# Holding the exponentials, and some row steps, while a gate bank's sums end, and spacing the copies of rpb

## The chip, the core and the metric

The kernel runs on one core of a Trainium2 chip. The core has a matrix engine (TensorE, PE in the profile; its weight loads are PEld), VectorE (DVE), ScalarE (ACT), GpSimd (POOL) and SyncE (SP), whose queue issues most transfers, and 16 DMA engines that the queues share. Each engine takes its instructions in program order and waits at one whose inputs are not there. The metric is the device time of one execution in microseconds, the median of several runs.

## The reference

One trunk layer is applied to 128 context tokens and 256 latent tokens, with the same weights and different conditioning:

```python
h = rms_norm(x, n1) * (1 + sc1) + sh1
q, k, v, u = project_in(h, w_in, q_g, k_g)       # 2048 -> 3*1024 + 1024
attn = attend(q, k, v)                           # 16 heads of 64
na = attn @ w_na_proj
fn = fourier_mix(u) @ w_fnet_proj
g_na, g_fn = split(sigmoid(h @ w_gate))          # 2048 -> 4096
x = x + g1 * ((g_na * na + g_fn * fn) @ w_o)
h2 = rms_norm(x, n2) * (1 + sc2) + sh2
x = x + g2 * swiglu(h2, w_gate_up, w_down)       # d_ff 5632
```

The shifts, scales and gates (sh1 to g2) come from silu(cond) @ w_mod, 2048 to 12288 wide. Context tokens attend to the context; latent tokens lie on a grid of 4 rows by 64 columns and attend, in one softmax, to a window of that grid with a bias table rpb, and to 128 cached keys. Keys and values of the context are outputs too.

## The kernel before, in words

**Products.** All weights are float32. A product of two float32 matrices is made as three matmuls of rounded halves (`mm3`, L147 to L149): high with high, high with low, low with high. Weights come in units of 256 rows by 512 columns: a load on SP's queue (`load_unit`, L187), then a split (`split`, L143 and L144): ScalarE casts the high half `wh`, VectorE subtracts it for the low half `wl`. `next_unit` gives the unit that is multiplied now; the unit that it splits is used two units later. `wh` and `wl` have three buffers each, the raw loads four.

**Work beside the products.** Everything else is written as generators which `Paced` steps at a rate per tick. `next_unit` has two ticks. The first one steps what is in the list `front`; then the split of a weight unit is issued; the second one steps `front` and `behind`. Inside the gate stage `mid_unit` gives a third tick to `front`, between the products of f = 0, 1 and those of f = 2, 3. I call the three A, B and C. Since all engines work in program order, the place of a step between these ticks sets its place in every engine's queue: what is issued on tick A stands ahead of the unit's split, what is issued on B or C stands behind it.

**Stages.** First come the modulation sums and the projection w_in in four groups of units (up to about 350 us). In the last group every unit multiplies for all tokens and the sums of a chunk of 512 columns are added up in SBUF (`acc`, L682); the sums of q, k, v, u go to DRAM (`s_qkvu`, written by `after`, L624 to L648). At the start of this group `expand_rpb` is put in `behind`: seven transfers from DRAM to DRAM (L250), each of which writes a slice of rpb 64 times over, so that the bias of a head pair can later be read as a slanted view (`bp`, L843).

Then comes the gate stage (about 350 to 690 us): eight banks of four sums (`po`, one PSUM tile for 128 gate columns by 384 tokens), each over eight units (u = 0, 2, ... 14). While the last unit is multiplied, each finished sum is copied to SBUF (`gst`, L1032): f = 0 and 1 on VectorE if one of the last three attention ticks held exponentials (`soft`), else on ScalarE; f = 2 and 3 on ScalarE. Four transfers on ScalarE's queue (L1035) store them. The next bank's first matmul needs the PSUM tile that the first copy frees.

Beside the gate products run, in `front`, the Fourier mixing and then the attention, in eight head pairs, and the row steps. The order of a pair is the table PAIR, fifteen ticks, that is five units:

```python
PAIR = "qk,b,pv,s0 m0,e0 i0,lq,s1 m1,e1 i1,,t0 lb,v,,t1,lv,"
```

`qk` transposes and splits q and k (L860 to L878), `b` masks the bias (L882), `pv` makes the products with v of the pair before (L976, L979, then L987 and L988), `s` makes scores (matmuls L893; then L905 on VectorE for the latent keys and L910, L914 on ScalarE for the others), `m` the maxima (L920, L924, VectorE), `e` the exponentials with their sums (L932, ScalarE), `i` the reciprocals (L940, VectorE) and the scaling (L942, ScalarE), `t` transposes (L958, TensorE) and splits (`pt`), `v` splits the values (L966, L967), and `lq`, `lb`, `lv` issue loads for the next pair. The digit is the tile of queries; s0 has four blocks of keys for each head pair to exponentiate, s1 two.

**Row steps.** Another part of the modulation is multiplied on VectorE: `accr` (L327, L329) takes one row block `wmr` of w_mod (loaded at L299) and adds it, times silu(cond), to a sum. `rows.rate` sets the steps per tick, and `rows.least` how much must be due before a tick does any.

Of the kernel before, what the change touches and what calls it, by code (L numbers as in the profile page):

```python
# [14 lines left out]
F32R = mybir.dt.float32r  # L15
# [4 lines left out]
P = 128  # L20
D = 2048
KT = D // P
# [79 lines left out]
def trunk_kernel(ctx: ExitStack, tc: tile.TileContext, io: dict):  # L102
# [35 lines left out]
    def nm(s):  # L138
        return f"{s}{next(ids)}"
# [6 lines left out]
    def mm3(out, aH, aL, bH, bL, start, stop):  # L146
        nc.tensor.matmul(out, aH, bH, start=start, stop=False)  # L147
        nc.tensor.matmul(out, aH, bL, start=False, stop=False)  # L148
        nc.tensor.matmul(out, aL, bH, start=False, stop=stop)  # L149

    def warm_sqrt():

        warm = small.tile([P, 1], F32, tag="warm", bufs=1, name=nm("warm"))
        nc.scalar.activation(out=warm, in_=ones[:, 0:1], func=AF.Sqrt)
# [53 lines left out]
    def next_unit():  # L208

        for p in front:  # L210
            p.tick()
        split_unit()
        for p in front + behind:
            p.tick()
        loads.more()
        return ready.popleft()
# [9 lines left out]
    qg8 = consts.tile([P, 1], F32, tag="qg8", name="qg8")  # L226
    rq = consts.tile([P, NT, NH], F32, tag="rq", name="rq")

    hH = [None] * KT
    hL = [None] * KT  # L230

    def new_h(kt):
        hH[kt] = hpool.tile([P, TOK], F32R, tag=f"tH{kt}", name=nm(f"hH{kt}_"))
        hL[kt] = hpool.tile([P, TOK], F32R, tag=f"tL{kt}", name=nm(f"hL{kt}_"))
        return hH[kt], hL[kt]

    s_qkvu = [dram.tile([P, NT, CH], F32, tag=f"sq{i}", name=f"s_qkvu{i}") for i in range(8)]
# [9 lines left out]
    def expand_rpb():  # L247
        for i in range(7):
            src = bass.AP(io["rpb"].tensor, (4 + i) * 31 + 15 - 63, [[465, NH], [0, 64], [1, P]])
            nc.sync.dma_start(s_rpb[i], src)  # L250
            yield
# [14 lines left out]
    with ExitStack() as ph:  # L266
# [170 lines left out]
        with ExitStack() as pha:  # L437
# [214 lines left out]
            for gi, (k0, n) in enumerate(GROUPS):  # L652
                prep.due, prep.rate = DUE[gi], PREP[gi]
                prep.least = 3.6 if gi else 1
                if gi == len(GROUPS) - 1:
                    behind.append(Paced(expand_rpb()))
                    new_ring()
                for rate, ci in zip(CHUNKS, ORDER):
                    if gi == len(GROUPS) - 1:
                        rows.rate = rate  # L660
                    po = [(mm_tile if gi < len(GROUPS) - 1 else acc_tile)() for _ in range(NT)]
                    if gi == 0:
                        acc[ci] = c6([P, NT, CH], "acc")
                    for u in range(k0, k0 + n, 2):
                        wH, wL = next_unit()
                        while prepared[0] < min(u + 2, k0 + n):
                            prep.step()
                        for t in range(NT):
                            sl = slice(t * P, (t + 1) * P)
                            for kk in range(min(k0 + n - u, 2)):  # L670
                                mm3(
                                    po[t], hH[u + kk][:, sl], hL[u + kk][:, sl], wH[:, kk], wL[:, kk],
                                    u + kk == k0, u + kk == k0 + n - 1,
                                )
                            if u + 2 >= k0 + n:
                                a = acc[ci][:, t]
                                if gi == 0 and t < 2:
                                    nc.scalar.copy(a, po[t])
                                elif gi == 0:
                                    nc.vector.tensor_copy(a, po[t])  # L680
                                else:
                                    nc.vector.tensor_add(a, a, po[t])  # L682
                    if gi == len(GROUPS) - 1:
                        behind.append(Paced(after(ci)))
# [128 lines left out]
                values()  # L813

        qks, vs, biases = [], [], []
        soft = deque(maxlen=3)

        def load_qk(hp):
# [27 lines left out]
        def attention_pair(hp, wk, values_before):  # L846
# [151 lines left out]
                    ("s", scores), ("m", maxima), ("e", exps), ("i", inverses), ("t", keys_first))},  # L998
            }
            for tick in PAIR.split(","):  # L1000
                for w in tick.split():
                    work[w]()
                soft.append("e" in tick)
                yield
# [13 lines left out]
        for fc8 in range(8):  # L1018
            po = [mm_tile() for _ in range(4)]
            sts = []  # L1020
            for u in range(0, KT, 2):
                wH, wL = next_unit()
                for f in range(4):
                    s = slice(f * P, (f + 1) * P)
                    if f == 2:
                        mid_unit()
                    for kk in range(2):
                        k = u + kk
                        mm3(po[f][:, :TOK], wH[:, kk, s], wL[:, kk, s], hH[k], hL[k], k == 0, k == KT - 1)
                    if u == KT - 2:  # L1030
                        st = gst.tile([P, TOK], F32, tag="st", name=nm("gst"))
                        (nc.vector.tensor_copy if f < 2 and any(soft) else nc.scalar.copy)(st, po[f][:, :TOK])  # L1032
                        sts.append(st)
            for f, st in enumerate(sts):
                nc.scalar.dma_start(s_gate[fc8][:, f], st)  # L1035
        br_work.drain()
        front.clear()
        behind.append(rows)
        pha.close()
# [368 lines left out]
```

## Time and profile before

| | |
|---|---|
| median of three runs | 2050.86 us (2049.79 to 2052.56) |
| profiled execution | 2052.19 us, span of the profile 2050.4 us |
| granted TensorE clock | 0.998 |
| TensorE busy, first 55 us | 41.95 us |
| TensorE busy, 55 to 350 us (w_in) | 291.82 of 295 us |
| TensorE busy, 350 to 700 us (gates, attention) | 346.80 of 350 us |
| VectorE busy, 350 to 700 us | 283.03 us |
| ScalarE busy, 350 to 700 us | 197.47 us |
| TensorE busy, 860 us to the end | 1186.01 of 1190 us |

A busy share says how much an engine works, not whether it is late. For that one reads the waits (who stood idle, and what instruction ended that) and the timeline, whose rows give start and duration in us, the engine, the line, the operation, and in brackets the idle time just before with its releaser.

### The profile page before, as it was taken

To read this page: it belongs to the slowest core of one execution; us is meant where nothing else is said; L and a number is where in the kernel's file an instruction comes from. 1 tells how busy PE (TensorE), PEld (TensorE's weight loads), DVE (VectorE), ACT (ScalarE), POOL (GpSimd) and SP (SyncE) were. 2 spreads that over 40 slices of the span, in tenths; PEclk is the share of its full clock that TensorE was granted. 3 is DMA by queue.
4 is the path that set the end of the run, shared out by engine and by line. 5 is a ranking of instruction groups with operands and counts; after the bars stand their busy time and mean duration, and the time that the engine had idled before them with its cause. 6 is when DMAs were issued, how large, how long until landed. Compare 5 with 4: busy or idle time off the path is not lost.

```text
span 2050.4 us, 27528 instructions
## 1 busy us (share of the span) xinstructions
PE 2025.8 (99%) x10986; PEld 1843.8 (90%) x10986; DVE 1248.0 (61%) x1528; ACT 757.9 (37%) x1135; POOL 43.1 (2%) x92
## 2 busy tenths in 40 slices
PE   7999999999999999999999999999999999999999
PEld 4668788999999999889998999899989998999897
DVE  4746889788987777765854444545454334333456
ACT  4433232456665434334523332222222232223222
POOL 1000000000001000010000000000000000000000
PEclk9999999999999999999999999999999999999999
DMA  9996979677776776754455555455554444444453
GB/s 332 328 338 222 309 232 315 215 217 212 228 212 181 258 248 194 250 168 154 124 167 156 152 163 155 144 153 155 155 163 134 124 129 127 129 128 123 136 163 123
DMA packets 220384, 390.46 MB, mean 190 GB/s; under 512 B 28464, under 2 KB 77632, under 8 KB 220256
## 3 DMA queue, kind: packets, MB, share of 16 engines
q1 hardware_dynamic: 213088, 382.13, 59.5%
q10 hardware_dynamic: 4672, 6.31, 0.9%
q8 instruction: 86, 1.41, 0.3%
q0 software_dynamic: 2496, 0.27, 0.1%
q14 instruction: 42, 0.34, 0.1%
HBM read 371.81 MB, written 20.51 MB: 191 GB/s over the span
## 4 chain that ended last, share of the span: by engine, by line
PE 94%; DMA 3%; DVE 2%; ACT 1%; issue 0%; SPq 0%; ACTq 0%; DVEq 0%
PE mm L147 19%; PE mm L149 19%; PE mm L148 19%; PE at L147 11%; PE at L149 11%; PE at L148 11%; PE at L404 1%; DMA wm<-in_w_mod 1%; DMA wraw<-in_w_in 1%; PE at L893 1%; PE at L979 1%; PE at L958 1%; DMA wmr<-in_w_mod 1%; DVE accr L329 0%; DMA xc<-in_x_prompt 0%
## 5 line engine op out<-in xcount | busy, mean ns | idle before, releaser
L144 DVE TENSOR_TENSOR wl<-wraw,wh 128x1024 fp32r<-128x1024 f32 (+1 forms) x464 | 559.1, 1205 | 668.5 <-ACT wh L143 667.3
L143 ACT CAST wh<-wraw 128x1024 fp32r<-128x1024 f32 (+1 forms) x464 | 480.9, 1038 | 1032.0 <-PE at L148 272.9
L147 PE MATMUL mm<-hH,wh 128*128 128x384 f32 x1152 | 389.4, 338 | 2.4 <-DVE gst L1032 2.4
L149 PE MATMUL mm<-hH,wl 128*128 128x384 f32 x1152 | 385.5, 335 | 0.0
L148 PE MATMUL mm<-hL,wh 128*128 128x384 f32 x1152 | 385.2, 334 | 0.0
L329 DVE SCALAR_TENSOR_TENSOR accr<-wmr,csz,accr 128x1024 f32<-128x1024 f32 x240 | 304.8, 1278 | 5.2 <-DMA wmr<-in_w_mod 5.1
L147 PEld LDWEIGHTS mm<-hH,wh 128*128 128x128 f32 x1152 | 216.3, 188 | 8.1 <-issue 4.3
L148 PEld LDWEIGHTS mm<-hL,wh 128*128 128x128 f32 x1152 | 216.4, 188 | 0.0
L149 PEld LDWEIGHTS mm<-hH,wl 128*128 128x128 f32 x1152 | 216.2, 188 | 0.0
L147 PE MATMUL at<-hH,wh 128*128 128x384 f32 x640 | 213.9, 334 | 0.0
L149 PE MATMUL at<-hH,wl 128*128 128x384 f32 x640 | 213.9, 334 | 0.0
L148 PE MATMUL at<-hL,wh 128*128 128x384 f32 x640 | 213.8, 334 | 0.0
L147 PE MATMUL mm<-wh,hH 128*128 128x512 f32 x404 | 160.8, 398 | 1.9 <-ACT hH L548 1.2
L148 PE MATMUL mm<-wl,hH 128*128 128x512 f32 x404 | 158.1, 391 | 2.8 <-DVE wl L144 2.8
L149 PE MATMUL mm<-wh,hL 128*128 128x512 f32 x404 | 158.4, 392 | 0.7 <-DVE hL L144 0.4
L147 PE MATMUL mm<-wh,cH 128*128 128x512 f32 x352 | 137.1, 389 | 0.0
L149 PE MATMUL mm<-wh,cL 128*128 128x512 f32 x352 | 137.0, 389 | 0.0
L148 PE MATMUL mm<-wl,cH 128*128 128x512 f32 x352 | 137.0, 389 | 0.0
L147 PEld LDWEIGHTS at<-hH,wh 128*128 128x128 f32 x640 | 120.1, 188 | 1.0 <-ACT wh L143 0.8
L148 PEld LDWEIGHTS at<-hL,wh 128*128 128x128 f32 x640 | 120.1, 188 | 0.2
L149 PEld LDWEIGHTS at<-hH,wl 128*128 128x128 f32 x640 | 120.1, 188 | 0.0
L147 PEld LDWEIGHTS mm<-wh,hH 128*128 128x128 f32 x404 | 76.0, 188 | 25.6 <-issue 3.1
(283 smaller groups left out, 2633.5 us busy)
## 6 DMA issues: line engine op xcount, KB each, us to landing
wraw<-in_w_gate_up SPq DMA_DIRECT2D x176, 512.0 KB, 3.7
wmr<-in_w_mod SPq DMA_DIRECT2D x128, 512.0 KB, 4.9
wraw<-in_w_down SPq DMA_DIRECT2D x88, 512.0 KB, 3.7
wraw<-in_w_gate SPq DMA_DIRECT2D x64, 512.0 KB, 4.3
wm<-in_w_mod SPq DMA_DIRECT2D x80, 384.0 KB, 6.7
wraw<-in_w_in SPq DMA_DIRECT2D x56, 512.0 KB, 5.8
wraw<-in_w_o SPq DMA_DIRECT2D x32, 512.0 KB, 4.7
wraw<-in_w_fnet_proj SPq DMA_DIRECT2D x16, 512.0 KB, 4.9
```

Source lines behind the costliest of these rows:

```text
L143: nc.scalar.copy(H, x)
L144: nc.vector.tensor_sub(L, x, fr(H))
L147: nc.tensor.matmul(out, aH, bH, start=start, stop=False)
L148: nc.tensor.matmul(out, aH, bL, start=False, stop=False)
L149: nc.tensor.matmul(out, aL, bH, start=False, stop=stop)
L329: nc.vector.scalar_tensor_tensor(out=acc[:, cnd], in0=wm, scalar=sc, in1=acc[:, cnd], op0=ALU.mult, op1=ALU.add)
L404: nc.tensor.matmul(pm[q : q + 32, :w], csz[:, k, :], wm[:, ty, kk + par, :], start=k < 2, stop=k >= KT - 2, tile_position=(0, q), skip_gro ...
L893: nc.tensor.matmul(po[j][:, cols], qx[rows[j], q], kx[rows[j], k], start=i == 0, stop=i == 2, tile_position=(j * HD, 0),)
L958: nc.tensor.transpose(o[:, i * P : (i + 1) * P], sc[:, j, c0 : c0 + P], ident)
L979: nc.tensor.matmul(po[j][:, CTX:TOK].rearrange("p (t q) -> p t q", t=2), w[1 + kc], x.rearrange("p (t b) q -> p t b q", t=2)[:, :, 2 * kc ...
```

## The change

It has three parts. The table of ticks, the rates and all the arithmetic are the same.

1. The transfers of `expand_rpb` are paced at 0.2 steps a tick, so that one goes every fifth unit and not one in each of the first seven.
2. While a bank's last unit (u = 14) is issued, `ending` is set. A tick of the attention that holds exponentials then yields instead, and comes at the first tick at which the flag is off, ahead of which no later step of the attention can go. In the same unit `rows.least` is 3, so that row steps wait; it is 1 again with the next unit and after the stage.
3. The high and low half of h share one tile of 2 x 384 columns. `hx`, a flat view of that tile, and `mm3_wide`, a product over it, are defined and not used.

```diff
+    def mm3_wide(out, aH, aL, b, start, stop):
+
+
+        nc.tensor.matmul(out, aH, b[:, :CH], start=start, stop=False)
+        nc.tensor.matmul(out[:, CH - TOK : TOK], aH, b[:, CH:], start=False, stop=False)
+        nc.tensor.matmul(out[:, :TOK], aL, b[:, :TOK], start=False, stop=stop)
+
...
+    hx = [None] * KT
     hH = [None] * KT
     hL = [None] * KT
 
     def new_h(kt):
-        hH[kt] = hpool.tile([P, TOK], F32R, tag=f"tH{kt}", name=nm(f"hH{kt}_"))
-        hL[kt] = hpool.tile([P, TOK], F32R, tag=f"tL{kt}", name=nm(f"hL{kt}_"))
+        h = hpool.tile([P, 2, TOK], F32R, tag=f"t{kt}", name=nm(f"h{kt}_"))
+        hH[kt], hL[kt] = h[:, 0], h[:, 1]
+        hx[kt] = h.rearrange("p i t -> p (i t)")
         return hH[kt], hL[kt]
...
-                    behind.append(Paced(expand_rpb()))
+                    behind.append(Paced(expand_rpb(), 0.2))
...
+        ending = [False]
         soft = deque(maxlen=3)
...
             for tick in PAIR.split(","):
+                while ending[0] and "e" in tick:
+                    yield
                 for w in tick.split():
                     work[w]()
                 soft.append("e" in tick)
...
             for u in range(0, KT, 2):
+                ending[0] = u == KT - 2
+                rows.least = 3 if ending[0] else 1
                 wH, wL = next_unit()
...
         br_work.drain()
+        rows.least = 1
```

**What moves.** The first held tick that changes the order lastingly is `e1 i1` of a pair at the end of bank 4; it moves from tick B of the last unit to tick A of the next, and the fifteen ticks of every later pair then fall two ticks later against the units. Here is ScalarE's queue in the pair after that, from the last instruction of the first scores on, before (`sc` holds the pair's scores, `mx` the maxima, `sm` the sums; `wh` is the high half of a weight unit):

```order
L914 ACTIVATE sc_4758<-at_4837,rq 128x128
L143 CAST wh_4859<-wraw_4612 128x1024
L932 ACTIVATE sc_4758,sm_4863<-sc_4758,mx_4856 128x384 x2
L932 ACTIVATE sc_4758,sm_4863<-sc_4758,mx_4856 128x128 x2
L942 ACTIVATE sc_4758<-sc_4758,sm_4863 128x384 x2
L942 ACTIVATE sc_4758<-sc_4758,sm_4863 128x128 x2
L910 ACTIVATE sc_4758<-at_4907,rq 128x128
```

And in the changed kernel, whose lines from here on are ten higher (L942 are the exponentials, L952 the scaling, L920 the copies of scores):

```order
L924 ACTIVATE sc_4763<-at_4842,rq 128x128
L942 ACTIVATE sc_4763,sm_4876<-sc_4763,mx_4861 128x384 x2
L942 ACTIVATE sc_4763,sm_4876<-sc_4763,mx_4861 128x128 x2
L952 ACTIVATE sc_4763<-sc_4763,sm_4876 128x384 x2
L952 ACTIVATE sc_4763<-sc_4763,sm_4876 128x128 x2
L143 CAST wh_4887<-wraw_4643 128x1024
L920 ACTIVATE sc_4763<-at_4910,rq 128x128
```

The cast `wh` stood ahead of the exponentials and now stands behind the scaling. VectorE's queue in the same pair, before, from the first maximum on (`accr` is a row step):

```order
L920 TENSOR_REDUCE mx_4856<-sc_4758 128x2
L924 TENSOR_REDUCE mx_4856<-sc_4758 128x2
L144 TENSOR_TENSOR wl_4860<-wraw_4612,wh_4859 128x1024
L940 RECIPROCAL sm_4863<-sm_4863 128x4
L329 SCALAR_TENSOR_TENSOR accr_4416<-wmr_4698,csz,accr_4416 128x1024
L905 SCALAR_TENSOR_TENSOR sc_4758<-at_4907,rq,bp_4670 128x256
L905 SCALAR_TENSOR_TENSOR sc_4758<-at_4908,rq,bp_4670 128x256
L920 TENSOR_REDUCE mx_4919<-sc_4758 128x2
L329 SCALAR_TENSOR_TENSOR accr_4416<-wmr_4698,csz,accr_4416 128x1024
L144 TENSOR_TENSOR wl_4923<-wraw_4683,wh_4922 128x1024
L940 RECIPROCAL sm_4926<-sm_4926 128x2
L329 SCALAR_TENSOR_TENSOR accr_4416<-wmr_4779,csz,accr_4416 128x1024
```

And in the changed kernel (L930 and L934 are the maxima, L950 the reciprocal, L915 the scores' work, L338 the row step):

```order
L930 TENSOR_REDUCE mx_4861<-sc_4763 128x2
L934 TENSOR_REDUCE mx_4861<-sc_4763 128x2
L950 RECIPROCAL sm_4876<-sm_4876 128x4
L338 SCALAR_TENSOR_TENSOR accr_4400<-wmr_4679,csz,accr_4400 128x1024
L144 TENSOR_TENSOR wl_4888<-wraw_4643,wh_4887 128x1024
L915 SCALAR_TENSOR_TENSOR sc_4763<-at_4910,rq,bp_4673 128x256
L915 SCALAR_TENSOR_TENSOR sc_4763<-at_4911,rq,bp_4673 128x256
L930 TENSOR_REDUCE mx_4922<-sc_4763 128x2
L338 SCALAR_TENSOR_TENSOR accr_4400<-wmr_4743,csz,accr_4400 128x1024
L950 RECIPROCAL sm_4939<-sm_4939 128x2
L144 TENSOR_TENSOR wl_4946<-wraw_4701,wh_4945 128x1024
L338 SCALAR_TENSOR_TENSOR accr_4400<-wmr_4743,csz,accr_4400 128x1024
```

Both reciprocals moved ahead of the weight half `wl` that stood in front of them, and the second scores' work L915 now comes right behind a `wl`. At the end of bank 6, later in the same stage, the copies of f = 0 and 1 were ScalarE's before; in the changed kernel they are on VectorE, behind the second scores of the pair, since the tick `e0 i0` is one of the last three:

```order
L144 TENSOR_TENSOR wl_5517<-wraw_5272,wh_5516 128x1024
L915 SCALAR_TENSOR_TENSOR sc_5390<-at_5539,rq,bp_5302 128x256
L915 SCALAR_TENSOR_TENSOR sc_5390<-at_5540,rq,bp_5302 128x256
L930 TENSOR_REDUCE mx_5551<-sc_5390 128x2
L338 SCALAR_TENSOR_TENSOR accr_4400<-wmr_5328,csz,accr_4400 128x1024
L144 TENSOR_TENSOR wl_5567<-wraw_5330,wh_5566 128x1024
L1046 COPY gst_5578<-mm_5111 128x384
L1046 COPY gst_5586<-mm_5112 128x384
L950 RECIPROCAL sm_5612<-sm_5612 128x2
```

The copies went to VectorE there, ahead of the held reciprocal. At bank 7's end it is the other way: f = 0 and 1 were VectorE's and are now ScalarE's.

## The prediction

> **What bounds the kernel now.** I read the page first, then the table of waits of TensorE, then the busy time in windows over the stages that the change touches, then the timeline around each stall found there. Three lines say what can be gained at all (the waits show engine, tile and line, the releaser, and microseconds in total, how often, the longest):
>
> ```profile
> PE 2025.8 (99%) x10986; PEld 1843.8 (90%) x10986; DVE 1248.0 (61%) x1528; ACT 757.9 (37%) x1135; POOL 43.1 (2%) x92
> ...
> PE mm L148 <- DVE wl L144: 2.8, 2, 2.0
> PE mm L147 <- DVE gst L1032: 2.4, 2, 1.5
> ```
>
> TensorE works 2025.8 of 2050.4 us, so every gain is one of its few waits. The change aims at two: a weight half `wl` that VectorE made late (2.0 us once), and the copy `gst` of a gate bank's sums on VectorE (1.5 us once, so 2.4 - 1.5 = 0.9 us the other time). Together 2.0 + 1.5 + 0.9 = 4.4 us is the most that it can win. The windows place them (columns: stretch and length, then busy us of PE, PEld, DVE, ACT, POOL, the granted clock, DMA share, GB/s):
>
> ```profile
> 220.00:230.00 10.00, 7.98 (x36) 6.31 (x35) 6.11 (x8) 2.72 (x3) 0.00 (x0) 1.00 0.77 280
> 500.00:510.00 10.00, 8.52 (x53) 8.22 (x52) 7.16 (x12) 7.85 (x18) 0.00 (x0) 1.00 1.00 302
> 630.00:640.00 10.00, 9.06 (x60) 8.16 (x59) 6.40 (x13) 6.22 (x19) 0.00 (x0) 1.00 0.48 146
> ```
>
> TensorE loses 2.02 us in the first (w_in, last group) and 1.48 and 0.94 in the others (ends of gate banks 4 and 7). What VectorE has to spare in the attention decides the rest. One window for each of five head pairs, from the start of its scores (L893) to the next pair's:
>
> ```profile
> 521.68:548.90 27.22, 27.22 (x178) 26.29 (x177) 24.76 (x33) 18.33 (x42) 0.00 (x0) 1.00 0.74 215
> 548.90:576.14 27.24, 27.24 (x178) 26.32 (x177) 25.40 (x35) 17.56 (x40) 0.00 (x0) 1.00 0.77 227
> 576.14:603.57 27.43, 27.43 (x178) 26.31 (x177) 24.56 (x32) 18.61 (x43) 0.00 (x0) 1.00 0.81 240
> 603.57:632.38 28.81, 28.81 (x187) 26.59 (x186) 18.77 (x30) 17.20 (x39) 5.35 (x11) 1.00 0.55 154
> 632.38:660.00 27.62, 26.68 (x172) 25.97 (x172) 23.10 (x31) 17.07 (x39) 0.00 (x0) 1.00 0.56 181
> ```
>
> The page's 61% hides this: in three pairs VectorE has 27.22 - 24.76 = 2.46, 1.84 and 2.87 us left.
>
> **The rpb transfers.** Seven are issued on SP's queue within 26 us, and here the late `wl` begins:
>
> ```profile
> L250 SPq DMA_DIRECT2D s_rpb<-in_rpb x7: 547/548/669, 182.5 to 208.1; - x7
> ...
> 200.00:210.00 10.00, 10.00 (x46) 8.29 (x45) 10.00 (x11) 2.73 (x3) 0.00 (x0) 1.00 1.06 351
> 210.00:220.00 10.00, 10.00 (x46) 8.29 (x45) 8.77 (x8) 2.11 (x2) 0.00 (x0) 1.00 1.04 368
> ...
> 222.83 1.05 ACT L143 CAST wh<-wraw 128x1024 fp32r<-128x1024 f32 x1 [4.61 <-DMA wraw<-in_w_in]
> 224.12 2.48 DVE L329 SCALAR_TENSOR_TENSOR accr<-wmr,csz,accr 128x1024 f32<-128x1024 f32 x2 [3.89 <-DMA wmr<-in_w_mod]
> 228.31 1.22 DVE L144 TENSOR_TENSOR wl<-wraw,wh 128x1024 fp32r<-128x1024 f32 x1
> 229.58 0.50 PE L148 MATMUL mm<-wl,hH 128*128 128x512 f32 x1 [2.02 <-DVE wl L144]
> ```
>
> The DMA engines are full (1.06 and 1.04); ScalarE waits 4.61 us for weights and VectorE 3.89 us for the matrix of a row step, and two row steps then run in a row ahead of `wl`. In the changed order a transfer goes every fifth unit (units 5, 10, ... 35 of the group), so that two of the seven, not seven, are in front of this place. I take the whole 2.0 us as won: no more is lost there, and if the first two alone filled the queue it would be 0. The other five transfers move to between about 240 and 315 us. What hides them is the margin of two units that `wl` has; the next crowded place is this one, and sets what they cost if that cover is gone:
>
> ```profile
> 330.00:340.00 10.00, 10.00 (x55) 9.41 (x54) 10.00 (x11) 3.16 (x3) 0.00 (x0) 1.00 1.03 376
> ...
> 334.29 1.05 ACT L143 CAST wh<-wraw 128x1024 fp32r<-128x1024 f32 x1 [1.77 <-DMA wraw<-in_w_gate]
> ```
>
> TensorE lost nothing there though ScalarE waited 1.77 us. The last transfer leaves about 15 us earlier, so I cost it at nothing, with 1.8 us as the upper end.
>
> **The h tiles and the row limit.** The two halves of h in one tile add no instruction and move none outside the gate stage; `mm3_wide` is never called and `hx` never read. I cost both at 0. The row limit holds row steps (1.3 us each on VectorE) for one unit of eight and then runs two at once: the same work, beside TensorE's, 0 unless VectorE is late already.
>
> **The held exponentials.** A tick that holds exponentials and falls into a bank's last unit now waits for the next unit. At bank 4 it was due on the second of the unit's three ticks, so that it slips by two ticks onto a first tick, and all later ticks of the attention keep that shift (their loads on SP's queue too, which go two ticks later as their users do, 0). Then, in every unit, `e0 i0` come ahead of the unit's weight split, where they came after it. The order shown above has it on both engines: ScalarE now runs four exponentials and four scalings and then `wh`; VectorE's reciprocal stands ahead of `wl`, and the second scores' work (L905) behind that `wl`. The pair at 521.68 as it was, in rows of the timeline (only those of VectorE, ScalarE and TensorE's scores and transposes that the sum uses):
>
> ```profile
> 521.62 0.44 PE L893 MATMUL at<-kH,qH 64*128 64x384 f32 x2
> ...
> 522.41 0.27 PE L893 MATMUL at<-kH,qL 64*128 64x128 f32 x2
> ...
> 523.72 0.88 DVE L905 SCALAR_TENSOR_TENSOR sc<-at,rq,bp 128x256 f32<-128x256 f32 x2
> ...
> 525.16 0.95 DVE L920 TENSOR_REDUCE mx<-sc 128x2 f32<-128x768 f32 x1 [0.56 <-ACT sc L910]
> 525.26 1.06 ACT L143 CAST wh<-wraw 128x1024 fp32r<-128x1024 f32 x1
> 526.03 0.41 DVE L924 TENSOR_REDUCE mx<-sc 128x2 f32<-128x256 f32 x1
> 526.20 0.64 ACT L932 ACTIVATE sc<-sc,mx 128x384 f32<-128x384 f32 x1
> 526.35 1.22 DVE L144 TENSOR_TENSOR wl<-wraw,wh 128x1024 fp32r<-128x1024 f32 x1
> ...
> 526.98 0.44 PE L893 MATMUL at<-kH,qH 64*128 64x384 f32 x2
> ...
> 528.08 0.20 ACT L932 ACTIVATION_READ_ACCUMULATOR sc<-sc,mx 128x1 f32 x1
> 528.31 0.18 DVE L940 RECIPROCAL sm<-sm 128x4 f32<-128x4 f32 x1 [0.74 <-ACT sc L932]
> 528.41 1.25 DVE L329 SCALAR_TENSOR_TENSOR accr<-wmr,csz,accr 128x1024 f32<-128x1024 f32 x1
> 528.53 1.71 ACT L942 ACTIVATE sc<-sc,sm 128x384 f32<-128x384 f32 x4 [0.24 <-DVE sm L940]
> ...
> 530.88 0.95 DVE L920 TENSOR_REDUCE mx<-sc 128x2 f32<-128x768 f32 x1 [0.43 <-ACT sc L910]
> ...
> 531.87 0.62 ACT L932 ACTIVATE sc<-sc,mx 128x384 f32<-128x384 f32 x1
> ...
> 532.99 0.19 ACT L932 ACTIVATION_READ_ACCUMULATOR sc<-sc,mx 128x1 f32 x1
> ...
> 534.28 1.12 ACT L942 ACTIVATE sc<-sc,sm 128x384 f32<-128x384 f32 x2 [1.10 <-DVE sm L940]
> ...
> 537.04 0.82 PE L958 MATMUL at<-ident,sc 128*128 128x128 f32 x6
> ```
>
> VectorE's idle time in the new order, wait by wait, with these durations: 0.56 before the first maximum, as now; from the second maximum's end (526.44) to the exponentials' end and the reciprocal (528.31) 1.87, since `wl` no longer fills it; then a row step to 529.66, while `wl` waits for the scalings' end (530.24) and a `wh` of 1.06, until about 531.2, so 1.5; 0.43 before the second maximum; 0.2 for the second reciprocal (it has a row step before it); and for the next `wl` the second scalings and a `wh`, 1.12 + 1.06 = 2.2, with the row step behind it in the queue and not ahead. Sum 6.8 us a pair, where 2.46 were free. Behind VectorE in that order stand `pt`, which TensorE needs for the products with v, and the maxima, so that its lateness reaches the transposes L958.
>
> Where VectorE's work and these waits exceed the pair's window, TensorE waits for the difference: 24.76 + 6.8 - 27.22 = 4.3; 25.40 + 6.8 - 27.24 = 5.0; 24.56 + 6.8 - 27.43 = 3.9; for the fourth 18.77 + 6.8 = 25.6 is under 28.81, nothing; for the fifth 23.10 + 6.8 - 27.62 = 2.3. Slack takes something off twice, at the start and after the fourth pair: VectorE's chain from L905 to the scalings' end ran 535.40 - 523.72 = 11.7 us. In the new order it is 2.7 (scores' work to the second maximum's end) + 1.9 (exponentials) + 1.9 (reciprocal, scalings) + 1.1 (`wh`) + 1.2 (`wl`) + 2.2 (second scores' work and maximum) + 1.3 (531.87 to 533.18, exponentials) + 0.2 + 1.1 (reciprocal, scalings) = 13.6; begun when the scores end (522.7) it ends at 536.3, 0.7 before L958 at 537.04. So 4.3 + 5.0 + 3.9 - 0.7 + 2.3 - 0.7 = 14.1 us. The bounds: 0, if the waits fall into time that VectorE has free in another order than I think, and 4.3 + 5.0 + 3.9 + 2.3 = 15.5 without slack. I take 14.1, near the upper end, because every one of these waits is a chain between the two engines and not a queue that can be worked off.
>
> At bank 4's end VectorE's copies now come ahead of the held reciprocal and the stall shrinks by about 0.5 of 1.5 us (it still has a weight half ahead of it); at bank 7's end all four copies go to ScalarE, and the 0.9 us go.
>
> **Sum.** Against the profiled execution of 2052.2 us: -2.0 - 0.5 - 0.9 + 14.1 = +10.7 us, 2062.9. That run lies 1.3 us over the median of the three, 2050.9, so the forecast on the median's footing is 2061.6 us. About 0.2%, 4.1 us, is what can be told from no change here.
>
> **The rivals.**
> First, the margin holds, and only gains are left. Each weight half is made two units ahead, the row steps can be late, and ScalarE is busy 18.33 us in 27.22. This decides if VectorE's true new idle time in a pair is under its 2.46, 1.84 and 2.87 free microseconds. Then -3.4 us, 2047.5; at most -4.4, 2046.5. Against it stands the sum of chained waits, more than twice that.
>
> Second, one place is late and not every pair: bank 6's end. There the new order puts `gst` on VectorE (it was on ScalarE) behind the whole chain: scores to second maximum 2.7, exponentials 1.8, reciprocal and scalings 1.9, `wh` 1.1, `wl` 1.2, second scores and maxima 2.3, a row step 1.2, `wl` 1.2, copy 0.5: 13.9 us after L905. The next bank's first matmul is due after the first scores (1.1 us), two and a half units (4.3 each, from 526.98 - 521.62 less 1.1) and the second scores (some 0.7), so 12.5 us after the scores' start, and L905 starts 1.1 to 2.1 us after that start. So 2.5 to 3.5 us are lost, say 2.9, and with the gains of 3.4 that is 2050.4, no change. It holds if lateness in the pairs is worked off between them.
>
> Third, the late rpb transfers collide with the stores of k and v: up to 1.8 us on top, 2063.4.
>
> Fourth, the clock drops after a long stall. The trace has such a place at its start:
>
> ```profile
> 10.00:20.00 10.00, 5.62 (x67) 3.98 (x65) 6.85 (x22) 7.13 (x19) 0.00 (x0) 0.98 1.12 303
> 20.00:30.00 10.00, 7.66 (x49) 4.13 (x51) 5.42 (x13) 3.37 (x8) 0.00 (x0) 0.68 1.06 357
> ```
>
> After 4.4 idle microseconds in pieces TensorE was granted 0.68 in the next 10 us, which costs 10 x (1 - 0.68) = 3.2 us; after the one stall of 2.02 us it kept 1.00. If one of my stalls of 4 to 5 us does the same, the time is 2061.6 + 3.2 = 2064.8, with two 2068.0. [...] My stalls are likely cut into several by the transposes and products of a pair, so I give this little.
>
> **How the numbers follow.** Main case 0.50; margin holds 0.22, half of it over the 0.2% (it would need nearly all of the 4.4 us); bank 6 alone 0.15; late transfers 0.05; clock 0.08. Slower: 0.50 + 0.05 + 0.08 + 0.01 = 0.64. Same: 0.11 + 0.14 = 0.25. Faster 0.11. The main case by itself spans 2054 (half of the 14.1) to 2063. The range runs from 2047.0, which leaves out the largest gains (some 0.08), to 2066.0, which leaves out repeated clock drops and other long stalls (some 0.1).
>
> **What would show it.** In the profile after: no wait for `wl` near 229 us (right for the rpb part); VectorE's table of waits with far more time for `wl` from `wh` and for the reciprocal (L950 there) from the exponentials; TensorE waiting for transposes' or products' inputs between 520 and 605 us, 3 to 5 us in each of three windows, and less from 605 to 632. If those windows show TensorE at full while VectorE idles 5 us or more, the chain has slack that I did not see, and the first rival is right. One wait of about 3 us for `gst` near 595 us alone is the second. A granted clock below 1.00 between 520 and 620 us is the fourth.

## The result, and the profile after

The changed kernel takes 2068.41 us (median of four runs, 2067.69 to 2071.71) against 2050.32 us for the kernel before on the same chips (2049.66 to 2052.56): a ratio of 1.0089, 95% interval 1.0072 to 1.0107. It is slower, as forecast, but by 18.1 us where 10.7 were forecast, and the time lies 2.4 us above the end of the range.

In the profiled executions the span went from 2050.4 to 2066.7 us, 16.3 more. First two lines of the changed kernel's page, what its engines were busy and the share of each in the chain of work that ended last:

```profile
PE 2031.5 (98%) x10986; PEld 1847.8 (89%) x10986; DVE 1247.7 (60%) x1528; ACT 759.3 (37%) x1135; POOL 43.1 (2%) x92
...
PE 89%; DVE 4%; ACT 3%; DMA 2%; issue 1%; SPq 1%; ACTq 0%; DVEq 0%
```

TensorE has the same 10986 matmuls, but is busy 5.7 us longer (2025.8 before). That leaves 16.3 - 5.7 = 10.6 us of additional waiting. (In the chain TensorE had 94% before, and VectorE 2%.) TensorE's waits in the changed kernel:

```profile
PE mm L147 <- DVE gst L1046: 6.8, 2, 5.9
PE at L968 <- ACT sc L952: 5.7, 7, 3.2
...
PE at L968 <- DVE pt L144: 1.1, 1, 1.1
...
PE at L989 <- DVE pt L144: 0.8, 1, 0.8
PE mm L148 <- DVE wl L144: 0.8, 1, 0.8
...
PE at L347 <- DVE pt L144: 0.4, 1, 0.4
...
PE at L986 <- DVE pt L144: 0.3, 1, 0.3
```

The 2.0 us for `wl` near 229 us are gone (the 0.8 that is left was there before, near 820 us). The two stalls for `gst` have changed: a small one of 0.9 at bank 4 and 5.9 us in one piece, at another bank. New are the waits for scaled scores (`sc`, L952) and for `pt`. The rows of the gate stage (all of these but `wl`) sum to 6.8 + 5.7 + 1.1 + 0.8 + 0.4 + 0.3 = 15.1 us; before, the three stalls that the change aimed at were 2.0 + 1.5 + 0.9 = 4.4. The difference is 10.7.

TensorE's timeline places the large ones (start, duration, operation, idle time before it and its releaser):

```profile
537.70 0.33 PE L968 MATMUL at<-ident,sc 128*128 128x128 f32 x1 [0.98 <-ACT sc L952]
...
569.92 1.83 PE L968 MATMUL at<-ident,sc 128*128 128x128 f32 x6 [3.17 <-ACT sc L952]
...
595.58 0.34 PE L149 MATMUL mm<-h,wl 128*128 128x384 f32 x1
601.78 0.66 PE L147 MATMUL mm<-h,wh 128*128 128x384 f32 x1 [5.87 <-DVE gst L1046]
602.24 0.53 PE L148 MATMUL mm<-h,wh 128*128 128x384 f32 x1
...
641.96 0.44 PE L968 MATMUL at<-ident,sc 128*128 128x128 f32 x2 [1.05 <-DVE pt L144]
669.80 0.33 PE L968 MATMUL at<-ident,sc 128*128 128x128 f32 x1 [0.85 <-ACT sc L952]
```

The matmul at 602.24 takes 0.53 us and not 0.34 as at 595.58. There most of the busy time was added. The windows around the two long stalls show why, in the column behind the engines, the granted clock:

```profile
566.00:576.00 10.00, 6.80 (x33) 6.19 (x32) 7.25 (x10) 8.17 (x16) 0.00 (x0) 0.83 0.50 159
598.00:608.00 10.00, 6.21 (x24) 6.15 (x25) 6.83 (x9) 5.38 (x12) 0.00 (x0) 0.66 0.71 223
220.00:230.00 10.00, 10.00 (x45) 8.26 (x44) 10.00 (x12) 1.68 (x2) 0.00 (x0) 1.00 0.83 269
500.00:510.00 10.00, 9.07 (x58) 8.72 (x57) 6.92 (x10) 6.74 (x14) 0.00 (x0) 1.00 0.74 226
630.00:640.00 10.00, 10.00 (x62) 9.43 (x63) 3.31 (x6) 6.79 (x16) 2.90 (x6) 1.00 0.19 56
```

At half speed 0.83 is 10 x 0.17 / 0.5 = 3.4 us, and 0.66 is 6.8 us: 10.2 us at half clock, worth up to 5.1 us (4.2 as the last part of the explanation works it out). The other three windows are those of before, where 2.02, 1.48 and 0.94 us were lost; now 0, 0.93 and 0.

VectorE's waits show the mechanism. Its timeline in the pair at bank 6's end, in the changed kernel (rows of VectorE alone):

```profile
588.00 0.88 DVE L915 SCALAR_TENSOR_TENSOR sc<-at,rq,bp 128x256 f32<-128x256 f32 x2
589.44 0.95 DVE L930 TENSOR_REDUCE mx<-sc 128x2 f32<-128x768 f32 x1 [0.56 <-ACT sc L920]
...
592.54 0.18 DVE L950 RECIPROCAL sm<-sm 128x4 f32<-128x4 f32 x1 [1.82 <-ACT sc L942]
...
595.44 1.23 DVE L144 TENSOR_TENSOR wl<-wraw,wh 128x1024 fp32r<-128x1024 f32 x1 [1.55 <-ACT wh L143]
...
597.89 0.95 DVE L930 TENSOR_REDUCE mx<-sc 128x2 f32<-128x768 f32 x1 [0.44 <-ACT sc L920]
...
601.09 1.02 DVE L1046 COPY gst<-mm 128x384 f32<-128x384 f32 x2
605.28 0.17 DVE L950 RECIPROCAL sm<-sm 128x2 f32<-128x2 f32 x1 [3.17 <-ACT sc L942]
```

The first four waits are 0.56, 1.82, 1.55 and 0.44, where 0.56, 1.87, 1.5 and 0.43 were worked out; the last one, 3.17, is that of the reciprocal held back at the bank's end. Two more waits, of 0.2 and 2.2 us, were worked out for a pair. They are seen in the first pair in the new order, whose first four waits are 0.56, 1.82, 1.54 and 0.44:

```profile
536.83 0.17 DVE L950 RECIPROCAL sm<-sm 128x2 f32<-128x2 f32 x1 [0.18 <-ACT sc L942]
539.12 1.23 DVE L144 TENSOR_TENSOR wl<-wraw,wh 128x1024 fp32r<-128x1024 f32 x1 [2.12 <-ACT wh L143]
```

Together that pair's six waits are 6.7 us, where 6.8 were worked out. From L915 at bank 6's end to the end of the first of the two copies it is 601.6 - 588.0 = 13.6 us.

### The profile page after: what moved, and what is told of

It reads as the page before. It is cut to its first block, busy times and chain, and to the rows that moved or that the text cites. A ratio compares the mean times of both kernels' runs of the same rounds, so it can differ in the third digit from the quotient of the medians.

```text
span 2066.7 us, 27541 instructions
## 1 busy us (share of the span) xinstructions
PE 2031.5 (98%) x10986; PEld 1847.8 (89%) x10986; DVE 1247.7 (60%) x1528; ACT 759.3 (37%) x1135; POOL 43.1 (2%) x92
## 4 chain that ended last, share of the span: by engine, by line
PE 89%; DVE 4%; ACT 3%; DMA 2%; issue 1%; SPq 1%; ACTq 0%; DVEq 0%
PE mm L147 18%; PE mm L149 18%; PE mm L148 18%; PE at L147 11%; PE at L149 11%; PE at L148 11%; PE at L413 1%; DVE wl L144 1%; DMA wm<-in_w_mod 1%; DVE accr L338 1%; ACT sc L942 1%; ACT wh L143 1%; ACT sc L952 1%; DVE mx L930 0%; ACT sc L920 0%
## 5 line engine op out<-in xcount | busy, mean ns | idle before, releaser
L147 PE MATMUL mm<-h,wh 128*128 128x384 f32 x1152 | 390.8, 339 | 6.8 <-DVE gst L1046 6.8
L149 PE MATMUL mm<-h,wl 128*128 128x384 f32 x1152 | 386.4, 335 | 0.0
L148 PE MATMUL mm<-h,wh 128*128 128x384 f32 x1152 | 386.3, 335 | 0.0
L338 DVE SCALAR_TENSOR_TENSOR accr<-wmr,csz,accr 128x1024 f32<-128x1024 f32 x240 | 304.3, 1278 | 0.1
L147 PEld LDWEIGHTS mm<-h,wh 128*128 128x128 f32 x1152 | 217.1, 188 | 12.5 <-issue 10.7
L148 PEld LDWEIGHTS mm<-h,wh 128*128 128x128 f32 x1152 | 217.2, 189 | 0.0
L149 PEld LDWEIGHTS mm<-h,wl 128*128 128x128 f32 x1152 | 217.0, 188 | 0.0
L147 PE MATMUL at<-h,wh 128*128 128x384 f32 x640 | 213.9, 334 | 0.0
L149 PE MATMUL at<-h,wl 128*128 128x384 f32 x640 | 213.9, 334 | 0.0
L148 PE MATMUL at<-h,wh 128*128 128x384 f32 x640 | 213.8, 334 | 0.0
L147 PE MATMUL mm<-wh,h 128*128 128x512 f32 x404 | 161.0, 399 | 1.9 <-ACT h L557 1.2
L148 PE MATMUL mm<-wl,h 128*128 128x512 f32 x404 | 158.2, 392 | 0.8 <-DVE wl L144 0.8
L149 PE MATMUL mm<-wh,h 128*128 128x512 f32 x404 | 158.5, 392 | 0.4 <-DVE h L144 0.4
L147 PEld LDWEIGHTS at<-h,wh 128*128 128x128 f32 x640 | 120.1, 188 | 1.0 <-ACT wh L143 0.8
L148 PEld LDWEIGHTS at<-h,wh 128*128 128x128 f32 x640 | 120.1, 188 | 0.2
L149 PEld LDWEIGHTS at<-h,wl 128*128 128x128 f32 x640 | 120.1, 188 | 0.0
```

What stands on the lines that cost most here:

```text
L338: nc.vector.scalar_tensor_tensor(out=acc[:, cnd], in0=wm, scalar=sc, in1=acc[:, cnd], op0=ALU.mult, op1=ALU.add)
```

## The experiments

Theory A is the prediction's: after the slip of two ticks the exponentials and scalings stand ahead of each weight split, and VectorE's work with the waits that come of it no longer fits into a pair. The rivals: B, another part of the change (spaced transfers, row limit, joint h tile) costs the time; C, the holds themselves do; D, the place of the ticks against the products does, not that of the split. Later ones ask how large each part is. The changed kernel's ratio is 1.0089; each ratio below is against the kernel before, run beside it, with its 95% interval.

| kernel | median us | before, beside it | ratio |
|---|---|---|---|
| hold alone | 2071.47 | 2050.93 | 1.0099 (1.0084 to 1.0114) |
| holds of whole units | 2054.36 | 2050.93 | 1.0013 (1.0003 to 1.0022) |
| split ahead of the first tick | 2054.06 | 2050.93 | 1.0012 (1.0003 to 1.0022) |
| slip from the fourth pair, no hold | 2067.20 | 2050.93 | 1.0079 (1.0064 to 1.0094) |
| spaced rpb alone | 2049.46 | 2052.18 | 0.9988 (0.9980 to 0.9997) |
| spaced rpb, row limit | 2050.68 | 2052.18 | 0.9995 (0.9986 to 1.0004) |
| changed, gst on ScalarE | 2064.32 | 2052.18 | 1.0063 (1.0047 to 1.0078) |
| changed, half the row steps there | 2108.27 (one execution) | 2052.18 | |
| spaced rpb, row limit in two banks | 2049.14 | 2051.72 | 0.9987 (0.9978 to 0.9995) |
| slip from the first pair, no hold | 2076.20 | 2051.72 | 1.0124 (1.0108 to 1.0139) |

**The hold alone.** The kernel before with this:

```diff
+        ending = [False]
...
             for tick in PAIR.split(","):
+                while ending[0] and "e" in tick:
+                    yield
...
+                ending[0] = u == KT - 2
                 wH, wL = next_unit()
```

> The kernel before with the hold of the exponentials alone (no spaced rpb transfers, no row limit, h in two tiles). Theory A (order: after the two-tick slip the exponentials and scalings stand ahead of each weight split, and each such pair costs TensorE time): the changed kernel's time plus the 2.0 us of the stall near 229 us that stays, 2068.4 + 2.0 = about 2070, with the same long waits of TensorE (about 3 us for the scaled scores near 570 us, about 6 us for gst near 600 us) and the clock at half after each. Theory B (the spaced transfers, the row limit or the joint h tile cost the time): within 3 us of the kernel before, 2048 to 2053.

2071.47 us: near theory A's number; B is out as the cause, since none of its parts is in this kernel. (What the joint h tile does by itself was not tested.) Its long waits are those of the changed kernel, 2.83 us for the scaled scores at 572.6 and 7.00 us for `gst` at 605.7 us. That the time comes out so near 2070 is in part luck: the wait near 229 us, taken at 2.0, was 0.6 us in this trace, and the copy at bank 4's end cost 2.14 us here and 0.93 in the changed kernel.

**Holds of whole units.** The changed kernel with this:

```diff
-                while ending[0] and "e" in tick:
+                held = 0
+                while (ending[0] and "e" in tick) or held % 3:
+                    held += 1
                     yield
```

> The changed kernel, but a hold always lasts a multiple of three ticks, a whole unit, so that after it the exponentials fall behind the weight split again as before. Holds are as many and longer. Theory A (order): the waits of each pair go; 2046 to 2053, granted clock 1.00 through the gate stage, VectorE's waits for wh and for the exponentials back near those of the kernel before. Theory C (the holds themselves cost: exponentials that come late make the transposes late at each bank end): as slow as the changed kernel or slower, 2068 to 2072.

14 us of the 18 are gone, with holds that are longer, not shorter: C is out as the cause of these 14. At 2054.4 it is 1 us above the band of A. Its table of waits says where:

```profile
PE mm L147 <- DVE gst L1048: 4.0, 2, 3.0
```

1.0 us of that is bank 4's and 3.0 bank 6's, where the hold still leaves `e0 i0` among the last three ticks, so that the copies stay on VectorE. The clock stayed at 1.00 here through the gate stage (1.00 from 350 to 700 us; what the mean of 0.997 lacks over the run, 6 us, is lost in the first 55 us, at 0.88).

**The split ahead of the first tick.** The changed kernel, its slip and its holds kept, and from bank 5 on:

```diff
+    split_first = [False]
+
...
+        if split_first[0]:
+            split_unit()
         for p in front:
             p.tick()
-        split_unit()
+        if not split_first[0]:
+            split_unit()
...
+            split_first[0] = fc8 >= 4
...
+        split_first[0] = False
```

> The changed kernel with its two-tick slip and its holds, but from bank 5 on the weight split is issued ahead of the unit's first tick, so that wh and wl stand between scores and exponentials again. Theory A (order of split and exponentials): 2046 to 2055, no long wait at 570 us, the gst wait near 600 us under 3 us. Theory D (the place of the ticks against the products, not the split, costs): 2063 or more.

2054.06 us, in A's band: the order of cast and exponentials, not the place of the ticks, is what costs; D is out. VectorE's waits from 510 to 690 us, first in the changed kernel, then in this one (whose lines are five higher), show what the order does:

```profile
DVE sm L950 <- ACT sc L942: 14.2, 10, 3.2
```

```profile
DVE sm L955 <- ACT sc L947: 2.7, 6, 0.8
```

The reciprocals wait 2.7 us for the exponentials and not 14.2; before it was 3.3. TensorE's large wait here is bank 6's `gst`, 2.6 us. The holds are not free, though: these two kernels (ratios 1.0013 and 1.0012) contain the spaced transfers and are still some 5 us slower than the kernel that has those alone (0.9988, below). In both, the copies at bank 6's end are on VectorE, and the row limit is in both; no run takes these last 5 us apart.

**The slip without a hold.** The kernel before with spaced transfers and this, for the fourth pair:

```diff
+                    if hp == 3:
+                        yield
+                        yield
                     values = yield from attention_pair(hp, wk, values)
```

> The kernel before with spaced rpb transfers and two empty ticks ahead of the fourth pair: the slip without any hold. Theory A (order): slow, since pairs four to eight run in the new order: 2060 to 2070. Theory C (the holds cost): no hold, so the time before less the 2.0 us of rpb, about 2048 to 2050.

2067.2 us: the slip alone is as slow as the whole change, without any hold. **From the first pair on**, with the two empty ticks ahead of the loop over pairs:

> The kernel before with the spaced rpb transfers and two empty ticks ahead of the first pair: all eight pairs in the new order, no hold. If each pair in that order costs by VectorE's account, the first three add 23.5 + 6.8 - 27.2, 24.7 + 6.8 - 28.5 and 24.5 + 6.8 - 29.0, together 8.4 us, to the run with the slip from the fourth pair on (2067.2): 2073 to 2077. If only bank 6's end and one pair ahead of it matter, nothing more: 2066 to 2069.

2076.2 us, 9.0 more than the run before it (8.4 were worked out; the two were timed on different chips, and the kernels beside them differ by 0.8). So the first three pairs, which the change leaves in the old order, would cost too: more pairs in the new order cost more. The size is not that of VectorE's account alone: from 350 to 700 us TensorE's waits are only 5.0 us more than in the run before (20.7 against 15.7), and the rest is longer busy time, with one more stretch of 3.4 us at half clock among it.

**Half the row steps in the gate stage.** The changed kernel with `RATES = [1.5, 0.25, ...]` in place of 0.5:

> The changed kernel with half the row steps in the gate stage; the others are done later, so that only the waits of the gate stage are read from this run. If VectorE's account decides (its work and its new waits exceed the pair's time), 2.5 row steps of 1.28 us less a pair give 3.2 us back, and TensorE's waits between 520 and 690 us, 14 us in the changed kernel, fall to 3 to 6 us, most of them at bank 6's end. If only the chain of waits decides, whatever else VectorE does, they stay above 10 us.

From 520 to 690 us TensorE waits 0.16 + 0.89 + 0.18 + 2.14 + 0.16 = 3.5 us where the changed kernel waited 13.5. VectorE's waits for the exponentials stay (14.2 us from 510 to 690 us, as in the changed kernel), and its work is less:

```profile
517.00:545.00 28.00, 27.84 (x179) 26.65 (x178) 18.48 (x28) 17.92 (x41) 0.00 (x0) 1.00 0.51 142
545.00:573.00 28.00, 26.93 (x173) 25.54 (x172) 20.07 (x28) 18.29 (x42) 0.00 (x0) 1.00 0.63 194
573.00:602.00 29.00, 26.86 (x157) 25.62 (x156) 20.31 (x30) 16.03 (x36) 0.00 (x0) 0.94 0.62 185
```

18.5 to 20.3 us of work and 6.8 of waits fit into 28 us. So VectorE's account decides, and not the length of one chain. (This is one execution, and its whole time, 2108.27 us, says nothing here: the row steps that were put off stop TensorE for 43.1 us near 960 us.)

**The copies on ScalarE.** The changed kernel with `nc.scalar.copy` for all of `gst`:

> The changed kernel with all gst copies on ScalarE. If the 5.9 us near 600 us are due to VectorE's lateness at that place (its copies stood behind two weight halves and two row steps), ScalarE's copies come at about 598.7 instead of 601.1 and the stall is about 3.3 us; with one clock window of 3.4 us less at half speed, 2068.4 - 2.6 - 1.7 = about 2064. If the whole stage is held up anyway and the wait only moves to the next transposes, no change, 2067 to 2069.

2064.32 us, as worked out, and its waits show it, the second row being bank 6:

```profile
PE at L968 <- ACT sc L952: 6.7, 10, 3.2
...
PE mm L147 <- ACT gst L1046: 3.0, 1, 3.0
```

5.87 us have become 2.99, and no clock is lost behind it: the first products behind it, from 601.51 us on, take 0.33 to 0.34 us each, where those from 602.24 us on took 0.53 in the changed kernel. In the new order the choice of the copying engine by the last three ticks costs time, but it is only a quarter to a third of the loss: 4.1 us between the two medians, 6.0 when each is compared with the kernel beside it. Whether the choice was right for the old order was not tested.

**The parts that win.** Spaced transfers alone, by the one line of the diff:

> The kernel before with the spaced rpb transfers alone. By the prediction the wait for wl near 229 us goes and nothing comes: 2.0 us less, 2048.9. If the late transfers collide with the stores of k and v (rival): a new wait of TensorE between 310 and 360 us and no gain, 2050 to 2051.

2049.46 us against 2052.18, a ratio of 0.9988: 2.5 us by the runs, with an interval of 0.6 to 4.1. In the trace the wait of 2.0 us is gone, and the span is 3.0 us shorter (2047.4 against 2050.4). From 310 to 360 us, where the last transfers now are, TensorE lost nothing:

```profile
310.00:360.00 50.00, 50.00 (x263) 45.41 (x262) 43.61 (x47) 14.84 (x16) 1.91 (x4) 1.00 0.94 323
```

With the row limit besides:

```diff
+                rows.least = 3 if u == KT - 2 else 1
                 wH, wL = next_unit()
```

> The kernel before with the spaced rpb transfers and the row limit in a bank's last unit, no hold. If the row limit is what helps the bank ends, the row steps ahead of gst at banks 4 and 7 (1.3 and 0.7 us) go and the stalls of 1.5 and 0.9 us shrink to about 0.3 each: 2050.9 - 2.0 - 1.8 = 2047.1. If two row steps in a row then make something else late (the changed kernel has waits of 0.2 and 0.4 us near 478 us), less: 2047.5 to 2049.

2050.68 us: the ratio's interval holds 1. Its trace shows both sides. The stalls at banks 4 and 7 are 0.28 us each, from 1.48 and 0.94; new are 0.18 and 0.43 near 478 us, and at bank 6 this:

```profile
PE mm L147 <- ACT gst L1033: 1.5, 1, 1.5
```

So 1.9 are won and 2.1 given back. **The row limit in banks 4 and 7 alone**, by `and fc8 in (3, 6)`:

> The kernel before with the spaced rpb transfers and the row limit only in the last units of banks 4 and 7, where gst waited for a row step. The row limit in all banks took 1.2 and 0.7 us there and gave 0.6 near 478 us and 1.5 at bank 6 back; without the other banks the first two stay: the spaced transfers alone, 2049.5, less 1.9 is 2047.6. If two row steps in a row after bank 4 carry on to bank 6's end, the 1.5 us come back and it is 2049.1.

2049.14 us: the second of the two expectations. The waits near 478 us are gone, bank 6's 1.45 us stays. This kernel and the one with the spaced transfers alone beat both the kernel before and the changed one, the former by about 0.1%; between the two of them nothing can be told (2.6 and 2.7 us under the runs beside them).

## Why the prediction was wrong in size, point by point

**Right: the direction, the mechanism and, in part by luck, the sum of waits.** The forecast was +14.1 us of new waits less 3.4 of gains, +10.7 together. The profiles show 16.3 us, of which TensorE's waits are 15.1 - 4.4 = 10.7. That the two sums agree to a tenth is luck: 0.6 of the 15.1 is due to the row limit, which was costed at nothing, and the pairs' shares came out otherwise. The step from the moved cast to VectorE's idle time came out wait by wait (0.56, 1.82, 1.54, 0.44, 0.18, 2.12), and four runs show that it is this order which costs: two that restore the old one win 14 of the 18 us back, two that only bring the new one about are slow by 16 and 24 us.

**Right: the gains.** The wait at 229 us went (2.0), bank 4's stall went from 1.48 to 0.93 (0.5), bank 7's went (0.9). The late transfers cost nothing. The wait at 229 us is not a fixed sum, though: it was 0.6 us in the trace of the hold alone, where the transfers are not spaced.

**Wrong: the clock.** This is the step that failed: "My stalls are likely cut into several by the transposes and products of a pair, so I give this little." They were not cut. One was 3.17 us and one 5.87 us in one piece, each brought the clock to half, for 3.4 and 6.8 us, and TensorE's busy time rose by 5.7 us for the same matmuls, of which the clock is about 4.2. The main case had put this term at nothing. The case "with two 2068.0" is near the time that was measured, but that is partly luck: it pays 2 x 3.2 = 6.4 us for two drops, and the 3.2 us come from a window that holds more than one drop, since in the kernel before the clock was at half from 19.66 to 23.08 and again from 26.49 to 29.90 us. The case had been given a share of 0.08 together with the single drop, and the range was cut at 2066.0 in front of it. A forecast of 4.3, 5.0 and 3.9 us of waits in three pairs, with 3.2 us for a drop taken from the trace, ought to have had at least one drop in its likeliest case: a sum of waits is not the end of it where the trace has shown the clock of the engine that waits fall beside idle time (0.68 from 20 to 30 us). The clock fell to half also in the run with the split ahead (0.94 in the window 576 to 605 us, that is 29 x 0.06 / 0.5 = 3.5 us), whose longest stall was 2.6 us, and in the run with half the row steps (0.94 in the window 573 to 602 us) after one of 2.1 us. It did not in the run with holds of whole units after one of 3.0 us; the last section shows where these stalls lay.

**Wrong: where the waits lie.** 4.3, 5.0, 3.9, 0 and 2.3 us were given to the five pairs, less 0.7 twice. In the order of time the profile has 0.98 + 0.18 + 0.28 = 1.4, 0.18 + 3.17 = 3.4, 5.87, 1.05 and 0.85 + 0.18 + 0.77 = 1.8. The lateness of the first pair is paid there only in part: VectorE carries it on, and most of it comes out later, 3.17 us at the transposes at 569.92 and 5.87 at the copies of bank 6, which TensorE needs at once. The second rival had priced that place at 2.9 us as if it stood alone, with L905 1.1 to 2.1 us after the scores' start; in the changed kernel L915 started 588.00 - 583.32 = 4.7 us after it (583.32 is the start of that pair's L903), and 13.6 + 4.7 - 12.5 = 5.8 is the stall that came. The two cases were not rivals, but one behind the other. The run with the copies on ScalarE shows how much hung on it: 4 to 6 us with the clock.

**Missed: the row limit.** It was costed at 0, "unless VectorE is late already". It is late already at two places: 0.6 us near 478 us and, without the hold, 1.5 us at bank 6.

How much of the 5.7 us of busy time is the clock can be worked out from windows of the traces. First the kernel before, from the start of the 1801st matmul to that of the 3890th, which takes in the gate stage:

```profile
362.80:700.40 337.60, 334.40 (x2091) 323.99 (x2091) 276.60 (x364) 192.77 (x402) 12.16 (x25) 1.00 0.71 216
```

Then the changed kernel between the same two matmuls by count, and its two stretches at half clock:

```profile
359.57:716.70 357.13, 341.12 (x2091) 327.22 (x2091) 275.80 (x364) 194.28 (x402) 12.16 (x25) 0.99 0.67 204
569.58:573.00 3.42, 3.05 (x11) 2.76 (x12) 2.48 (x3) 3.42 (x7) 0.00 (x0) 0.50 0.00 0
600.30:603.72 3.42, 1.94 (x6) 1.97 (x7) 1.80 (x3) 0.00 (x0) 0.00 (x0) 0.50 0.36 53
603.72:607.13 3.41, 3.41 (x15) 3.32 (x14) 1.85 (x3) 2.96 (x7) 0.00 (x0) 0.50 1.02 356
```

In this stage TensorE is busy 341.12 - 334.40 = 6.7 us longer. At half clock it was busy 3.05 + 1.94 + 3.41 = 8.4 us; half of that, 4.2 us, is the price of the clock by the granted share. What stays open is the other 2.5 us, for which the forecast had no term either, and with it whether each stall costs some busy time besides.

## What to carry to other kernels

When work is interleaved by ticks, a wait that holds a step back for a number of ticks that is not a whole period changes the order of everything behind it, for good; look in the order for what the shift has put between a producer and its consumer on another engine, and hold for whole periods. An engine that is 61% busy over the kernel can have no room in one stage: add the waits that a new order forces to its work in one period, and compare with the period. If the sum is over, the lateness can pile up until an urgent instruction on that engine shows it, as the copies at bank 6's end did here (5.87 us), and such a stall of TensorE can be paid again in its clock: here 4.2 us with stalls of 3.17 and 5.87 us.

## What had not been expected of the hardware

The granted clock fell to half for 3.4 us with stalls of 2.1, 2.6 and 3.2 us and for 6.8 us with one of 5.9 us, and stayed at 1.00 with stalls of 2.0 and 3.0 us. So in these runs the length of a stall alone doesn't say whether the clock falls. What the traces show besides is when it changes: in the changed kernel's gate stage at 569.58, 573.00, 600.30 and 607.13 us, of which the last three lie 1, 9 and 11 times 3.413 us behind the first, and in the first 30 us of the kernel before at 19.66, 23.08, 26.49 and 29.90 us, 1, 2 and 3 times 3.413 us behind the first. I call a stretch of 3.413 us between two such times a slot. Here is the slot ahead of the first drop in the changed kernel:

```profile
566.17:569.58 3.41, 0.58 (x4) 0.26 (x2) 1.60 (x4) 2.13 (x7) 0.00 (x0) 1.00 0.74 276
```

In the run with holds of whole units, the two slots that the stall of 3.0 us lies in:

```profile
587.92:591.33 3.41, 2.10 (x13) 1.77 (x11) 2.98 (x5) 3.41 (x8) 0.00 (x0) 1.00 0.68 193
591.33:594.75 3.42, 1.73 (x10) 1.76 (x11) 3.42 (x5) 0.58 (x2) 0.00 (x0) 1.00 0.71 141
```

In the run with half the row steps, the slot with the stall of 2.1 us and the one behind it:

```profile
586.69:590.10 3.41, 1.27 (x7) 0.98 (x7) 2.80 (x4) 1.37 (x3) 0.00 (x0) 1.00 0.54 159
590.10:593.51 3.41, 3.41 (x15) 3.31 (x14) 0.68 (x2) 1.79 (x5) 0.00 (x0) 0.50 0.88 282
```

The stall of 3.0 us was shared by two slots with 1.3 and 1.7 us idle, and the clock stayed. The stall of 2.1 us fell into one slot, and the next slot was at half clock. The run with the copies on ScalarE has a second case of a stall that was shared: its matmuls go from 0.52 us at 575.18 to 0.34 us at 575.75, so that its clock changes in between; 7 times 3.413 us later, at 599.4 to 599.6 us, TensorE was in the stall of 2.99 us (598.24 to 601.23), and the clock stayed. The other slot at full clock that was followed by half clock in the changed kernel, and then the slots at full clock that were not and had the most idle time in the gate stages of the kernel before and of the changed one:

```profile
596.89:600.30 3.41, 0.00 (x0) 0.00 (x0) 2.97 (x5) 2.43 (x5) 0.00 (x0) 1.00 0.55 156
504.35:507.77 3.42, 2.23 (x13) 2.23 (x14) 1.60 (x3) 1.58 (x5) 0.00 (x0) 1.00 1.00 292
535.45:538.86 3.41, 2.25 (x15) 1.74 (x14) 1.36 (x3) 3.14 (x7) 0.00 (x0) 1.00 0.63 248
```

So slots with 2.14, 2.83 and 3.41 us idle were followed by half clock, and slots with 1.16, 1.19, 1.31 and 1.69 us idle were not; these rows show nothing between 1.7 and 2.1 us. The slots lie differently against the kernel's start from run to run: near 590 us a slot ends at 590.06 us in the changed kernel (569.58 + 6 x 3.413), at 590.10 in the run with half the row steps and at 591.33 in that with holds of whole units. A stall of 2 to 3 us was followed by half clock in some of these runs (2.1 and 2.6 us) and not in others (2.0, 2.99 and 3.0 us).
